# Turning feed-forward activations with 32x32 block transposes and a trip through DRAM

## The chip, the cores and the metric

The kernel runs on one core of a Trainium2 chip. The metric is the device time of one execution in microseconds (us). TensorE (PE) does the matrix products, VectorE (DVE) and ScalarE (ACT) the elementwise work, GpSimd (POOL) a few small operations, and SyncE (SP) issues the DMAs. Sixteen DMA engines move data between DRAM (HBM) and the on-chip memory; all queues share them.

## The reference

Two transformer blocks of two layers each run one after the other on one sequence of 256 positions, width 1024, in fp32. Block 1 has in each layer a SwiGLU feed-forward, a mixer with three attention branches, and a second SwiGLU feed-forward; block 2 has in each layer a mixer with two attention branches and a squared-ReLU feed-forward. What matters here are the feed-forwards:

```
# block 1, four times (width 2816)
g, u = split(h @ w_gu);  x = x + 0.5 * ((silu(g) * u) @ w_down)
# block 2, twice (width 4096)
u = square(relu(h @ w_up));  x = x + gt2 * (u @ w_down)
# once, for block 2: mod = silu(c) @ w_ada + b_ada   (c is one vector)
```

## The kernel before, in words

**Arithmetic.** A product in fp32 is done as three matmuls in a shorter format (fp32r). Each operand is split into a high part (`Copy` on ACT into fp32r) and a low part (original minus high part, on DVE), and PE adds hi x hi, hi x lo and lo x hi (L1238, L1239, L1240).

**Blocks, pieces, units.** Every weight product is a `Block`: 512 output columns (or fewer) and all of K. A block is cut into pieces of two 128-row slices of K; a piece is done for the first half of the tokens (t = 0) and then for the second (t = 1), and each of these is a unit: two slices of three matmuls, six matmuls of 512 columns. Weights arrive in groups of four slices (1 MB) in one of four `raw` buffers (L1132, issued by SP), are split per piece into one of eight `whi` (L1159, ACT) and one of eight `wlo` buffers (L1157, DVE), and the split of a piece is written out six pieces ahead of its use.

**The order of the work** is a stream written out by a generator program. Before each unit, `step()` advances every running chain (a Python generator that writes instructions) by one; `yield n` in a chain means that it goes on n units later. If the activations that a unit needs are not yet written in the program, `step()` is called again until they are (L1224 to L1229). All engines execute in the order of the program, each on its own queue, and wait for each other by semaphores.

**Activations.** The left operand of a product has to have the K dimension on the partitions, so each result of 128 tokens x 512 columns (a strip, for one t) is turned: four 128x128 transposes on PE into one PSUM bank (`transposes`, L206), then `HT.put` writes the high part (ACT, L226) and the low part (DVE, L228). In the SwiGLU a strip j costs two blocks, one for the gate (silu on ACT, L404) and one for the up columns (product on DVE, L409). There are five strips of 512 columns and one of 256, whose gate and up columns share a block. In block 2 the width is done in two parts of 2048 columns; a part has four strips j (relu L1042 and square L1043 on ACT), and then a down product of two blocks over the part's K (added to x at L1024 and L1025). A down block reads strip 0 first, then 1, 2, 3 and so on.

**Chores.** During the feed-forwards of block 1 the program also computes `mod`: 192 loads of 256 KB of `w_ada` on SP's queue (L330), alternately two and three units apart. Each is multiplied into an accumulator on DVE (L345, L347); that instruction is written after the next load's, about five units after its own load.

**Memory.** Temporaries of up to 2 KB per partition come from one pool of 18 slots (`slab2`), taken and given back in the order of the program.

Of the kernel before, what the change touches and what calls it, by code (L numbers as in the profile page):

```python
# [7 lines left out]
F32 = mybir.dt.float32  # L8
F32R = mybir.dt.float32r
BF16 = mybir.dt.bfloat16  # L10
I32 = mybir.dt.int32
AF = mybir.ActivationFunctionType
# [4 lines left out]
D = 1024  # L17
# [7 lines left out]
NBUF = 8  # L25
NRAW = 4
NS4 = 14
NS2 = 18
LEAD = 6
SKEW_2 = 7  # L30
SKEW_1 = 6
# [7 lines left out]
UP_WAIT = 2  # L39
ACT_WAIT = 3  # L40
P_WAIT = 4
MERGE_WAIT = 3
PT_WAIT = 3
ROPE_WAIT = 5
# [20 lines left out]
def tile_kernel(ctx: ExitStack, tc: tile.TileContext, a, out, stages=99):  # L65
    nc = tc.nc
    V, S, T, G = nc.vector, nc.scalar, nc.tensor, nc.gpsimd

    def pool(name, bufs, **kw):
        return ctx.enter_context(tc.tile_pool(name=name, bufs=bufs, **kw))  # L70

    const = pool("const", 1)
# [5 lines left out]
    small = pool("small", 6)  # L78
    mmp = pool("mmp", 3, space=PSUM)
    trp = pool("trp", 5, space=PSUM)  # L80
    dram = pool("dram", 1, space=bass.MemoryType.DRAM)
    ctx.enter_context(tc.manual_schedule())

    def slab4(shape, dt=F32):
# [2 lines left out]
    def slab2(shape, dt=F32):  # L87
        return s2p.tile(shape, dt, name="s2", tag="s2")
# [8 lines left out]
    def bc(ap, shape):  # L97
        return ap.to_broadcast(shape)

    def tk(t):  # L100
        return slice(t * 128, (t + 1) * 128)
# [2 lines left out]
    x = [const.tile([128, D], F32, name=f"x{t}") for t in range(2)]  # L104
    ident = const.tile([128, 128], F32, name="ident")
    cols = const.tile([128, NCOLS], F32, name="cols")
    tri = const.tile([128, 512], F32, name="tri")
    nhalf = const.tile([128, 32], F32, name="nhalf")
    identb = const.tile([128, 128], BF16, name="identb")
    masks = const.tile([128, 5, 128], BF16, name="masks")  # L110
    trir = const.tile([128, 2, 128], F32R, name="trir")
    rope1 = const.tile([128, 2, 2, 16], F32, name="rope1")
# [12 lines left out]
    def setup_late():  # L125
        yield 10
        S.activation(csil, cols[:, COLS["c_2"]:COLS["c_2"] + 8], AF.Silu)
        spawn(chores())
        mk = slab2([128, 3, 128])
        pi = small.tile([128, 2], I32, name="pi")  # L130
        pf = small.tile([128, 2], F32, name="pf")
        inv = small.tile([128, 32], F32, name="inv")
        for dst, src in ((tri, a["tri"]), (mk, a["masks"]), (rope1, a["rope1"]), (pi, a["pos"]), (inv, bc(a["inv"][None, :], [128, 32]))):
            nc.sync.dma_start(out=dst, in_=src)
            yield 2
        for l in range(2):
            for c, n, nm in ((0, 6, "b_forget"), (8, 8, "swa_sinks_2"), (32, 64, "g_idx_k")):
                nc.sync.dma_start(out=rowb[:, l, c:c + n], in_=row(nm, l, n))
                yield 2
        yield 8  # L140
        V.memset(masks[:, 0], 0.0)
        V.tensor_copy(masks[:, 1:3], mk[:, 0:2])
        V.tensor_copy(masks[:, 3], mk[:, 0])
        V.tensor_copy(masks[:, 4], mk[:, 2])
        V.tensor_copy(trir, tri[:, 256:512].rearrange("p (a b) -> p a b", a=2))
        V.tensor_copy(identb, ident)
        for l in range(2):
            V.tensor_scalar(rowb[:, l, 16:24], rowb[:, l, 8:16], -1.0, None, op0=ALU.mult)
        V.tensor_copy(pf, pi)
        w = slab2([128, 3, 2, 32])  # L150
        ang, n, nh = w[:, 0], w[:, 1], w[:, 2]
        for t in range(2):
            V.tensor_scalar(ang[:, t], inv, pf[:, t:t + 1], None, op0=ALU.mult)
        for first in (True, False):
            V.tensor_scalar(n, ang, 0.15915494309189535, MAGIC, op0=ALU.mult, op1=ALU.add)
            V.tensor_scalar(n, n, -MAGIC, None, op0=ALU.add)
            if first:
                V.tensor_scalar(nh, n, 1.0 / 4096, MAGIC, op0=ALU.mult, op1=ALU.add)
                V.tensor_scalar(nh, nh, -MAGIC, 4096.0, op0=ALU.add, op1=ALU.mult)
                V.tensor_sub(n, n, nh)  # L160
            for c in TWO_PI:
                if first:
                    V.scalar_tensor_tensor(ang, nh, -c, ang, op0=ALU.mult, op1=ALU.add)
                V.scalar_tensor_tensor(ang, n, -c, ang, op0=ALU.mult, op1=ALU.add)
            yield 2
        V.tensor_scalar(nh, ang, 1.5707963267948966, None, op0=ALU.add)
        V.tensor_scalar(n, nh, PI, -6.283185307179586, op0=ALU.is_gt, op1=ALU.mult)
        V.tensor_add(nh, nh, n)
        V.tensor_scalar(nh, nh, PI, -PI, op0=ALU.min, op1=ALU.max)
        V.tensor_scalar(ang, ang, PI, -PI, op0=ALU.min, op1=ALU.max)  # L170
        S.activation(sin2[:, :, 0], nh, AF.Sin)
        S.activation(sin2[:, :, 1], ang, AF.Sin)
        spawn(launcher())
# [29 lines left out]
    def transposes(src, n=128):  # L203
        pt = trp.tile([128, 4, 128], F32, name="tr")
        for i, s in enumerate(src):
            T.transpose(pt[:n, i, :], s, ident)  # L206
        return pt

    def chunks(src, k):
        return [src[:, i * 128:(i + 1) * 128] for i in range(k)]  # L210

    class HT:


        def __init__(self, sizes=None):
            self.q, self.done = {}, set()
            self.at = [(i, j) for i, n in enumerate(sizes or [4] * 8) for j in range(n)]

        def tile(self, i):
# [4 lines left out]
        def put(self, i, t, src, n=4):  # L224
            h, l = self.tile(i)
            S.activation(h[:, :n, tk(t)], src, AF.Copy)  # L226
            yield 1
            V.tensor_sub(l[:, :n, tk(t)], src, h[:, :n, tk(t)].bitcast(F32))  # L228
            self.done.add((i, t))

        def ready(self, kc, t):
            return (self.at[kc][0], t) in self.done
# [15 lines left out]
    plan = []  # L248
# [146 lines left out]
    def plan_ffn(l, prep, w_gu, w_down, nxt, before_down=None):  # L395
        sizes = [4, 4, 4, 4, 4, 2]
        aT = HT(sizes)
        for j in range(6):
            n, c0 = sizes[j] * 128, sum(sizes[:j]) * 128
            sg = {}  # L400

            def silu(t, ps, n=n, sg=sg):
                sg[t] = slab2([128, 512])
                S.activation(sg[t][:, :n], ps[:, :n], AF.Silu, scale=prep.r[t])  # L404
                yield

            def mul(t, ps, n=n, sg=sg, j=j):
                act = slab2([128, 512])
                V.scalar_tensor_tensor(act[:, :n], ps[:, :n], prep.r[t], sg.pop(t)[:, :n], op0=ALU.mult, op1=ALU.mult)  # L409
                yield ACT_WAIT  # L410
                pt = transposes(chunks(act, n // 128))
                yield 1
                yield from aT.put(j, t, pt[:, :n // 128], n // 128)

            def both(t, ps, silu=silu, mul=mul):
                yield from silu(t, ps[:, 0:256])
                yield from mul(t, ps[:, 256:512])

            if n == 256:
                plan.append(Block(w_gu[l], D, c0, 512, prep.hT, both, second=DFF + c0))  # L420
            else:
                plan.append(Block(w_gu[l], D, c0, n, prep.hT, silu, skew=SKEW_1 * (j == 0)))
                plan.append(Block(w_gu[l], D, DFF + c0, n, prep.hT, mul))
        if before_down:
            before_down()
        for nh in range(2):
            def add(t, ps, nh=nh):
                xs = x[t][:, nh * 512:(nh + 1) * 512]
                V.scalar_tensor_tensor(xs, ps, 0.5, xs, op0=ALU.mult, op1=ALU.add)  # L429
                yield from nxt.half(t, nh)  # L430

            if nh and nxt.kind == "final":
                plan.append(lambda: busy.append(1))
            plan.append(Block(w_down[l], DFF, nh * 512, 512, aT, add))
# [601 lines left out]
    def plan_mlp2(l, prep, gt, nxt, before_down=None, cuts=(0, 512, 1024)):  # L1036
        for part in range(2):
            uT = HT()
            for j in range(4):
                def up(t, ps, j=j, uT=uT):  # L1040
                    u = slab2([128, 512])
                    S.activation(u, ps, AF.Relu)  # L1042
                    S.activation(u, u, AF.Square)  # L1043
                    yield UP_WAIT
                    pt = transposes(chunks(u, 4))
                    yield 1
                    yield from uT.put(j, t, pt)

                plan.append(Block(a["w_up_2"][l], D, part * 2048 + j * 512, 512, prep.hT, up, skew=SKEW_2 * (part == 0 and j == 0)))
            if part and before_down:  # L1050
                before_down()
            plan_res(a["w_down_2"][l][part * 2048:(part + 1) * 2048], 2048, uT, gt, nxt if part else None, cuts if part else (0, 512, 1024))
# [4 lines left out]
    p = p_ffn[0]  # L1057
    for l in range(2):
# [3 lines left out]
        p = Prep(1, gcol("g_ffn2", l))  # L1062
# [14 lines left out]
        p = q  # L1077
# [38 lines left out]
    i = 0  # L1116
# [190 lines left out]
```

## Time and profile before

| | us |
|---|---|
| median of 3 runs | 1912.08 (1912.01 to 1912.32) |
| the profiled execution, its own time | 1911.74 |
| its span, first to last instruction | 1910.0 |
| PE busy | 1888.1 (99%) |
| DVE busy | 1305.8 (68%) |
| ACT busy | 1040.4 (54%) |
| granted TensorE clock | 1.00 throughout |

Busy time is the time in which an instruction of the engine ran; the issuing of DMAs isn't counted in it. Matmuls overlap each other, so PE's pace is better read from the distances between the starts of its instructions than from their durations. SPq marks the queue of SP, on which a DMA issue has a start and a duration of its own, apart from the time that the transfer takes.

### The profile page before, as it was taken

What the parts mean: (1) busy time and instruction counts of PE and PEld (TensorE: products, weight loads), DVE (VectorE), ACT (ScalarE), POOL (GpSimd) and SP (SyncE); (2) the same over time, 40 slices, a digit from 0 to 9 for tenths busy, and PEclk for the clock granted to TensorE, in tenths of its full rate; (3) what the DMA queues carried; (4) which work ended last, traced back from release to release, by engine and by line L of the source; (5) the groups of instructions that cost most, each with busy time, mean ns of one, the idle gap of its engine ahead of it and who ended that gap; (6) DMA issues with size and microseconds to landing.
All of it is one profiled execution on the core that took longest, in us unless ns stands there. A gap on an engine that the chain in (4) does not pass through costs nothing.

```text
span 1910.0 us, 24975 instructions
## 1 busy us (share of the span) xinstructions
PE 1888.1 (99%) x9300; PEld 1557.6 (82%) x9300; DVE 1305.8 (68%) x2231; ACT 1040.4 (54%) x1622; POOL 68.4 (4%) x84
## 2 busy tenths in 40 slices
PE   8999999999999999999999999999999999999999
PEld 6888987888888888897888888877888887788888
DVE  6876775577677776684757775886855479767454
ACT  5444576555444544466655443677464547656452
POOL 0000100000000000000000000110000012000000
PEclk9999999999999999999999999999999999999999
DMA  9777553558776877563456775644665645456552
GB/s 316 264 266 244 158 170 118 177 184 278 259 262 232 286 250 253 192 186 116 143 193 242 265 264 175 200 154 133 205 214 177 218 138 177 154 177 210 187 165 78
DMA packets 212041, 385.73 MB, mean 202 GB/s; under 512 B 12008, under 2 KB 43752, under 8 KB 211920
## 3 DMA queue, kind: packets, MB, share of 16 engines
q1 hardware_dynamic: 211920, 384.14, 60.3%
q8 instruction: 73, 1.20, 0.3%
q14 instruction: 48, 0.39, 0.1%
HBM read 382.96 MB, written 1.15 MB: 201 GB/s over the span
## 4 chain that ended last, share of the span: by engine, by line
PE 92%; DVE 4%; ACT 3%; issue 1%; DMA 0%; SPq 0%; POOL 0%; ACTq 0%
PE mm L1238 28%; PE mm L1240 28%; PE mm L1239 28%; PE tr L206 4%; PE tr L448 1%; DVE wlo L1157 1%; ACT whi L1159 1%; PE tr L517 1%; PE tr L519 0%; DVE s L903 0%; PE tr L361 0%; DMA x<-in_x_dram 0%; DVE s L852 0%; ACT s L470 0%; ACT s L696 0%
## 5 line engine op out<-in xcount | busy, mean ns | idle before, releaser
L1238 PE MATMUL mm<-whi,s 128*128 128x512 f32 (+3 forms) x2600 | 1011.0, 389 | 1.3 <-ACT s L404 1.2
L1240 PE MATMUL mm<-whi,s 128*128 128x512 f32 (+3 forms) x2600 | 989.2, 380 | 0.4 <-DVE s L228 0.3
L1239 PE MATMUL mm<-wlo,s 128*128 128x512 f32 (+3 forms) x2600 | 987.7, 380 | 1.0 <-DVE wlo L1157 1.0
L1157 DVE TENSOR_TENSOR wlo<-raw,whi 128x1024 fp32r<-128x1024 f32 (+4 forms) x657 | 751.3, 1159 | 281.7 <-ACT whi L1159 279.8
L1159 ACT ACTIVATE whi<-raw 128x1024 fp32r<-128x1024 f32 (+4 forms) x657 | 644.9, 1004 | 267.8 <-PE mm L1240 252.9
L1238 PEld LDWEIGHTS mm<-whi,s 128*128 128x128 f32 x2600 | 489.4, 188 | 98.5 <-issue 13.4
L1240 PEld LDWEIGHTS mm<-whi,s 128*128 128x128 f32 x2600 | 488.8, 188 | 93.0 <-DVE s L228 1.4
L1239 PEld LDWEIGHTS mm<-wlo,s 128*128 128x128 f32 x2600 | 489.7, 188 | 84.2 <-DVE wlo L1157 1.9
L347 DVE SCALAR_TENSOR_TENSOR s<-s,csil,s 128x512 f32<-128x512 f32 x168 | 125.6, 747 | 56.6 <-DMA s<-in_w_ada_dram 56.6
L226 ACT ACTIVATE s<-tr 128x512 fp32r<-128x512 f32 (+1 forms) x112 | 64.3, 580 | 106.0 <-PE tr L206 106.0
L206 PE MATMUL tr<-ident,s 128*128 128x128 f32 x734 | 110.1, 274 | 5.8 <-ACT s L786 2.6
L206 PEld LDWEIGHTS tr<-ident,s 128*128 128x128 f32 x734 | 88.5, 141 | 28.9 <-issue 7.3
L262 ACT ACTIVATE s<-x 128x512 bf16<-128x512 f32 x44 | 27.7, 630 | 124.8 <-DVE x L429 56.4
L228 DVE TENSOR_TENSOR s<-tr,s 128x512 fp32r<-128x512 f32 (+1 forms) x112 | 73.2, 666 | 4.3 <-ACT s L226 3.9
L404 ACT ACTIVATE s<-mm,prep 128x512 f32<-128x512 f32 (+1 forms) x48 | 31.3, 653 | 79.0 <-PE mm L1240 78.0
L409 DVE SCALAR_TENSOR_TENSOR s<-mm,prep,s 128x512 f32<-128x512 f32 (+1 forms) x48 | 33.8, 704 | 43.6 <-PE mm L1240 38.2
L268 POOL TENSOR_TENSOR prep<-prep,nhalf 128x1 f32<-128x1 f32 x18 | 16.9, 937 | 1059.6 <-DVE prep L267 1059.6
L456 DVE CUSTOM_DVE_ANT_0 s<-tr,masks 128x128 f32<-128x128 f32 x88 | 27.7, 353 | 30.4 <-PE tr L448 30.4
L1024 DVE TENSOR_TENSOR s<-mm,s 128x512 f32<-128x512 f32 (+1 forms) x26 | 16.8, 647 | 46.1 <-PE mm L1240 46.1
L1042 ACT ACTIVATE s<-mm 128x512 f32<-128x512 f32 x32 | 19.1, 597 | 41.7 <-PE mm L1240 40.3
L226 ACT ACTIVATE s<-s 128x512 fp32r<-128x512 f32 x24 | 14.9, 630 | 40.9 <-DVE s L317 40.9
L820 ACT ACTIVATE s<-mm,prep 128x512 f32<-128x512 f32 x24 | 16.5, 688 | 34.7 <-PE mm L1240 32.4
(206 smaller groups left out, 900.1 us busy)
## 6 DMA issues: line engine op xcount, KB each, us to landing
raw<-in_w_ffn_gu_dram SPq DMA_DIRECT2D x79, 1024.0 KB, 5.9
raw<-in_w_in_dram SPq DMA_DIRECT2D x56, 1024.0 KB, 5.2
s<-in_w_ada_dram SPq DMA_DIRECT2D x192, 256.0 KB, 5.9
raw<-in_w_ffn_down_dram SPq DMA_DIRECT2D x40, 1024.0 KB, 5.3
raw<-in_w_up_dram SPq DMA_DIRECT2D x32, 1024.0 KB, 5.4
raw<-in_w_down_dram SPq DMA_DIRECT2D x28, 1024.0 KB, 5.2
raw<-in_w_out_dram SPq DMA_DIRECT2D x16, 1024.0 KB, 5.1
raw<-in_w_in_dram SPq DMA_DIRECT2D x16, 640.0 KB, 4.0
```

The costliest lines, as they stand in the source:

```text
L206: T.transpose(pt[:n, i, :], s, ident)
L226: S.activation(h[:, :n, tk(t)], src, AF.Copy)
L228: V.tensor_sub(l[:, :n, tk(t)], src, h[:, :n, tk(t)].bitcast(F32))
L262: S.activation(slab2([128, 512], BF16), x[t][:, nh * 512:(nh + 1) * 512], AF.Square, scale=1.0 / 32, accum_out=self.ms[:, t, o + nh:o + nh ...
L347: V.scalar_tensor_tensor(accs[0], raw, c, accs[0], op0=ALU.mult, op1=ALU.add)
L404: S.activation(sg[t][:, :n], ps[:, :n], AF.Silu, scale=prep.r[t])
L409: V.scalar_tensor_tensor(act[:, :n], ps[:, :n], prep.r[t], sg.pop(t)[:, :n], op0=ALU.mult, op1=ALU.mult)
L1157: V.tensor_sub(lo[:pr, d, :b.n], src, h.bitcast(F32))
L1159: S.activation(h, src, AF.Copy)
L1238: T.matmul(ps, xh, hi[:, i, :b.n], start=(k == 0), stop=False)
L1239: T.matmul(ps, xh, lo[:, i, :b.n], start=False, stop=False)
L1240: T.matmul(ps, xl, hi[:, i, :b.n], start=False, stop=(k == len(b.rows) - 1))
```

## The change

For the strips of 512 columns of the SwiGLU (five of six, four times) and for two of the four strips in each part of block 2's feed-forward, the transposes on PE go. DVE transposes the strip in 32x32 blocks inside the on-chip memory, one instruction for each t; ACT's queue issues a DMA that writes the 256 KB to DRAM. When both t are written, ACT's queue issues four DMAs that read the strip back in the turned order (128 KB each, one for each quarter of the partitions) into one buffer `back`. Then ACT makes the high part and DVE the low part from `back`. `BLOCK_WAITS` holds the distances in units: 2 from the transpose to the write, 9 from the write of t = 1 to the reads, 9 from the reads to the high part. A list `landing` lets one strip at a time be between its reads and its low parts. In block 2 the strips are computed in the order 2, 3, 0, 1, and strips 2 and 3, which the down block reads last, take the new way. To make room, some constants move to the pool, which has 17 slots instead of 18.

```diff
-NS2 = 18
+NS2 = 17
...
+BLOCK_WAITS = (2, 9, 9)
...
+    blocksp = pool("blocksp", 4, space=bass.MemoryType.DRAM)
+    backp = pool("backp", 1)
...
-    tri = const.tile([128, 512], F32, name="tri")
+    tri = const.tile([128, 256], F32, name="tri")
...
+        def put_blocks(self, i, t, src):
+            turned = slab2([128, 512])
+            V.transpose(turned, src.rearrange("p (c j a) -> p j c a", j=4, a=32))
+            if t == 0:
+                self.blocks[i] = blocksp.tile([128, 4, 2, 128], F32, name="d")
+            d = self.blocks[i]
+            yield BLOCK_WAITS[0]
+            nc.scalar.dma_start(out=d[:, :, t], in_=turned.rearrange("p (j e) -> p j e", j=4))
+            if t == 0:
+                return
+            yield BLOCK_WAITS[1]
+            while landing:
+                yield 1
+            landing.append(1)
+            back = backp.tile([128, 4, 2, 128], F32, name="back")
+            for j in range(4):
+                nc.scalar.dma_start(out=back[32 * j:32 * j + 32], in_=self.blocks[i].rearrange("(i a) j t e -> j a i (t e)", a=32)[j])
+            yield BLOCK_WAITS[2]
+            h, l = self.tile(i)
+            for u in range(2):
+                x_, hu, lu = back[:, :, u].rearrange("p i (c s) -> p c i s", s=32), *(z[:, :, tk(u)].rearrange("p c (i s) -> p c i s", s=32) for z in (h, l))
+                S.activation(hu, x_, AF.Copy)
+                yield 1
+                V.tensor_sub(lu, x_, hu.bitcast(F32))
+                self.done.add((i, u))
+            landing.clear()
...
             def mul(t, ps, n=n, sg=sg, j=j):
                 act = slab2([128, 512])
                 V.scalar_tensor_tensor(act[:, :n], ...)
+                if n == 512:
+                    yield 1
+                    yield from aT.put_blocks(j, t, act)
+                    return
                 yield ACT_WAIT
...
-            for j in range(4):
+            for j in (2, 3, 0, 1):
                 def up(t, ps, j=j, uT=uT):
                     u = slab2([128, 512])
                     S.activation(u, ps, AF.Relu)
                     S.activation(u, u, AF.Square)
                     yield UP_WAIT
+                    if j > 1:
+                        yield from uT.put_blocks(j, t, u)
+                        return
                     pt = transposes(chunks(u, 4))
```

## Rows read from the trace of the kernel before

**Rows 1.** Head of the page: span; busy time, share of the span, instructions.

```profile
span 1910.0 us, 24975 instructions
PE 1888.1 (99%) x9300; PEld 1557.6 (82%) x9300; DVE 1305.8 (68%) x2231; ACT 1040.4 (54%) x1622; POOL 68.4 (4%) x84
```

**Rows 2.** Chain that ended last, share of the span by engine.

```profile
PE 92%; DVE 4%; ACT 3%; issue 1%; DMA 0%; SPq 0%; POOL 0%; ACTq 0%
```

**Rows 3.** What PE waited for, whole span: total us, times, longest.

```profile
PE mm L1239 <- DVE wlo L1157: 1.0, 1, 1.0
```

**Rows 4.** Timeline of ACT, second feed-forward: start, duration, instruction, idle before and releaser.

```profile
531.55 1.06 ACT L1159 ACTIVATE whi<-raw 128x1024 fp32r<-128x1024 f32 x1 [1.66 <-PE mm L1240]
```

**Rows 5.** Timeline of PE around one group of four transposes, first feed-forward.

```profile
61.62 0.40 PE L1240 MATMUL mm<-whi,s 128*128 128x512 f32 x1
61.86 0.60 PE L206 MATMUL tr<-ident,s 128*128 128x128 f32 x4
62.21 0.48 PE L1238 MATMUL mm<-whi,s 128*128 128x512 f32 x1
62.53 0.40 PE L1239 MATMUL mm<-wlo,s 128*128 128x512 f32 x1
```

**Rows 6.** Timeline of DVE, feed-forward of block 2, layer 0.

```profile
1410.66 0.68 DVE L228 TENSOR_TENSOR s<-tr,s 128x512 fp32r<-128x512 f32 x1
...
1422.48 0.68 DVE L228 TENSOR_TENSOR s<-tr,s 128x512 fp32r<-128x512 f32 x1
...
1440.44 0.69 DVE L1024 TENSOR_TENSOR s<-mm,s 128x512 f32<-128x512 f32 x1 [4.48 <-PE mm L1240]
...
1462.20 0.69 DVE L1024 TENSOR_TENSOR s<-mm,s 128x512 f32<-128x512 f32 x1 [4.48 <-PE mm L1240]
```

**Rows 7.** Groups by shape: count, total busy us, mean ns, idle before.

```profile
L228 DVE TENSOR_TENSOR s<-tr,s 128x512 fp32r<-128x512 f32 x104 | 69.8, 685 | 4.3 <-ACT s L226 3.9
L226 ACT ACTIVATE s<-tr 128x512 fp32r<-128x512 f32 x104 | 61.2, 595 | 97.2 <-PE tr L206 97.1
L228 DVE TENSOR_TENSOR s<-s,s 128x512 fp32r<-128x512 f32 x24 | 16.2, 688 | 5.1 <-ACT s L226 4.9
L226 ACT ACTIVATE s<-s 128x512 fp32r<-128x512 f32 x24 | 14.9, 630 | 40.9 <-DVE s L317 40.9
L345 DVE TENSOR_SCALAR s<-s,csil 128x512 f32<-128x512 f32 x24 | 11.6, 483 | 6.0 <-DMA s<-in_w_ada_dram 6.0
```

**Rows 8.** Stretches: busy us by engine, clock, DMA share, GB/s (strips 1 to 5; start).

```profile
410.00:530.00 120.00, 120.00 (x558) 98.60 (x557) 87.94 (x104) 61.55 (x74) 2.04 (x2) 1.00 0.73 249
15.00:17.50 2.50, 2.50 (x14) 2.09 (x13) 2.50 (x4) 1.75 (x4) 0.00 (x0) 1.00 1.06 387
```

**Rows 9.** Timeline of SP's queue, second feed-forward: issues.

```profile
544.34 0.38 SPq L1132 DMA_DIRECT2D raw<-in_w_ffn_down_dram  x1
544.83 0.92 SPq L330 DMA_DIRECT2D s<-in_w_ada_dram  x2
```

**Rows 10.** The same at the start of the kernel.

```profile
15.70 11.19 SPq L1132 DMA_DIRECT2D raw<-in_w_ffn_gu_dram  x4
```

**Rows 11.** DMA issues: count, KB each, median us from issue to landing.

```profile
s<-in_w_ada_dram SPq DMA_DIRECT2D x192, 256.0 KB, 5.9
...
out_dram<-x SPq DMA_DIRECT2D x4, 128.0 KB, 1.7
```

**Rows 12.** Timeline of ACT, feed-forward of block 2: relu and square of a strip.

```profile
1417.74 0.60 ACT L1042 ACTIVATE s<-mm 128x512 f32<-128x512 f32 x1 [3.02 <-PE mm L1240]
1418.37 0.63 ACT L1043 ACTIVATE s<-s 128x512 f32<-128x512 f32 x1
```

**Rows 13.** What DVE waited for between 410 and 530 us.

```profile
DVE wlo L1157 <- ACT whi L1159: 10.2, 7, 3.2
DVE s L409 <- PE mm L1240: 9.7, 3, 4.5
DVE s L347 <- DMA s<-in_w_ada_dram: 7.9, 5, 3.5
```

More of the change, by code (lines that the diff above doesn't have):

```diff
@@ L129, in setup_late @@
         mk = slab2([128, 3, 128])
[L130 to L133, printed above, removed]
+        pi = slab2([128, 2], I32)
+        late = slab2([128, 2, 128])
+        pfi = slab2([128, 34])
+        pf, inv = pfi[:, 0:2], pfi[:, 2:34]
+        for dst, src in ((tri, a["tri"][:, 0:256]), (late, a["tri"][:, 256:512].rearrange("p (a b) -> p a b", a=2)), (mk, a["masks"]), (rope1, a["rope1"]), (pi, a["pos"]), (inv, bc(a["inv"][None, :], [128, 32]))):
             nc.sync.dma_start(out=dst, in_=src)
@@ L144, in setup_late @@
         V.tensor_copy(masks[:, 4], mk[:, 2])
-        V.tensor_copy(trir, tri[:, 256:512].rearrange("p (a b) -> p a b", a=2))
+        V.tensor_copy(trir, late)
         V.tensor_copy(identb, ident)
@@ L210, in chunks @@
         return [src[:, i * 128:(i + 1) * 128] for i in range(k)]
+    landing = []
     class HT:
         def __init__(self, sizes=None):
-            self.q, self.done = {}, set()
+            self.q, self.done, self.blocks = {}, set(), {}
             self.at = [(i, j) for i, n in enumerate(sizes or [4] * 8) for j in range(n)]
@@ L1047, in up @@
                     yield from uT.put(j, t, pt)
-                plan.append(Block(a["w_up_2"][l], D, part * 2048 + j * 512, 512, prep.hT, up, skew=SKEW_2 * (part == 0 and j == 0)))
+                plan.append(Block(a["w_up_2"][l], D, part * 2048 + j * 512, 512, prep.hT, up, skew=SKEW_2 * (part == 0 and j == 2)))
             if part and before_down:
```

## The prediction

> **What bounds the kernel now.** I read the head of the page first: PE is busy for 1888.1 of 1910.0 us, DVE for 68% and ACT for 54% [rows 1]. Busy matmuls can hide waiting, so I looked next at the chain that ended last: 92% of it is PE [rows 2]. Then at what PE waits for: a low weight part was late once in the whole span, by 1.0 us [rows 3]. And then at ACT, which feeds DVE: in the steady stream it finishes a `whi` and stands 1.66 us until PE gives a buffer back [rows 4]. So the splits run as far ahead as the buffers let them, and the time is the sum of what PE executes. What takes instructions off PE is worth its full length, as long as the others still keep ahead.
>
> **Part 1: the transposes that go.** Between the starts of the last matmul before a group of four and the second one after it lie 0.91 us [rows 5]; without the group it would be two steps. A step I take from a down block without transposes: the two halves of x, one block of 16 units apart, lie at 1440.44 and 1462.20, so 21.76 us for 16 units or 1.36 for a unit of six matmuls, 0.227 each [rows 6]. The group costs 0.91 - 0.45 = 0.46. The other way: two strips of block 2 in succession are 11.82 us apart (1410.66 to 1422.48) and hold 8 units and two groups [rows 6]: (11.82 - 10.88) / 2 = 0.47. I take 0.47.
> Groups that go: 5 strips x 2 t x 4 SwiGLUs = 40, and 2 strips x 2 t x 2 parts x 2 layers = 16; together 56, so PE loses 56 x 0.47 = 26.3 us.
> The Trainium skill speaks against it: "VectorE: DVE Perf Modes", Rules for kernel authors, sends a 128x128 transpose to TensorE and keeps DVE's for 32x32 blocks, and its section on the three transpose paths gives 390 ns for one on TensorE (bf16). Here four take 0.47 us in fp32, so the row is cheaper than the page; by its figure 56 x 4 x 0.39 = 87 us would go. The rule leaves out that PE is the only full engine here, and the row decides.
>
> **Part 2: DVE.** It gains 56 block transposes; the two low parts of a strip stay, from memory instead of PSUM (688 against 685 ns) [rows 7]. No row shows a block transpose. The nearest from below is a one-source operation of the same shape, 483 ns; from above two passes of a two-stream one, 2 x 688 = 1.38 us [rows 7]. I take 0.69, one element a step as in the two-stream rows. In the strips of a SwiGLU DVE is busy for 87.94 of 120 us [rows 8]. A strip takes 16 x 1.36 + 2 x 0.47 = 22.70 us now, 16.6 of them busy; afterwards 16.6 + 2 x 0.69 = 18.0 of 21.76 (83%), or 19.4 (89%) at the upper bound. It is off the path either way, at 0 us.
>
> **Part 3: ACT.** The high parts cost 630 instead of 595 ns [rows 7], 2 us in all, hidden. New are the issues on its queue: 2 writes and 4 reads for each of 28 strips, 168. No row shows an issue on ACT. SP's take 0.38 us for 1 MB and 0.46 for 256 KB [rows 9]; with 4 MB queued at the start they took 11.19 / 4 = 2.8 [rows 10]. I take 0.46, since the stream in between is the first kind, and keep 2.8 as the far end; the lower end is 0. ACT in a strip: 61.55 / 120 x 22.70 = 11.6 us, then 11.6 + 6 x 0.46 = 14.4 of 21.76; it keeps its lead. At 2.8 it would be 28.4 and ACT the bound (below).
>
> **Part 4: are the activations in time?** In units after the end of a strip's t = 1 (U) the program of the SwiGLU writes: product at 1, block transpose at 2, DMA write at 4, reads at 13, high part at 22, low parts at 23 and 24. The last strip of this kind has 8 units of strip 5 and 16 units of the down block in front of it and is needed from U + 25: two units to spare at t = 0 and at t = 1. The write waits on ACT for DVE's transpose only, and the reads wait for the write. A store of 128 KB landed after 1.7 us [rows 11]; nine units are 12.2 us, so neither wait holds up the `whi` queued behind it. The next strip's reads come at 29, when `landing` is empty since 24. Cost 0.
> The Trainium skill, "DMA: Bandwidth & Descriptors", section on two DMAs through the same engine, says that only the first one's completion makes it safe to read what it wrote; the 1.7 us row is that completion for half the bytes, and no run here shows the read behind it.
> In block 2 it is tighter. Relu and square at 1, transpose 3, write 5, reads 14, low parts 24 and 25; strip 3 finds `landing` taken until U + 25 of strip 2, so its reads are written in the very unit in which strip 1's t = 1 is evicted, and in front of it on ACT. They also wait for DVE's last low part of strip 2, because there is one `back`. Relu and square start up to 1.8 us (four issues) and about 1 us for that low part late, and PE's transposes of strip 1 are written only two units (2.72 us) behind, of which relu and square need 1.23 [rows 12]. So 2.8 + 1.23 - 2.72 = 1.3 us of PE wait, once in the second part of each layer: 2 x 1.3 = 2.6. In the first part seven pieces are skewed, the collision falls on the high part of strip 1, which has four units until it is read, and strip 3's low part is written one `step()` late, both behind data already landed: 0. Without the new order strips 2 and 3 would be the ones next to the down block; with it strip 1 keeps PE's transposes and is ready one unit ahead.
>
> **Part 5: the small edits.** The constants move at the start, on SP, where PE waits for x and weights; the pool with 17 slots, now with `turned` held until its write has landed, can make a later user wait. No row prices that: between -1 and +2 us, since the one wait of PE above is of that size [rows 3]; I take 0.
>
> **Sum.** 1911.74 (the profiled execution) - 26.3 + 2.6 = 1888.0; the median of the runs shown lies 0.34 above that execution, so 1888.4 in the terms of the median. Forecast 1888.5, with a range of its own from 1885 to 1893.
>
> **Rivals.**
> A. *ACT's issues cost more than SP's, or the read data come late.* For it: ACT would execute them between splits, which SP doesn't do, and no row shows it. At 1.2 us each a burst of four is 4.8 instead of 1.8, so each of the four parts of block 2 loses about 3 us more, 12 in all: 1888.5 + 12 = 1900.5. Against it: the strips of block 1 have two units to spare and ACT 7 us of each strip.
> B. *Slower: the chores' loop in the SwiGLUs becomes the bound.* SP takes its next load when DVE has finished a `wlo`; the `w_ada` load behind it lands, and DVE stands at the accumulation, written about five units after the load. DVE waits there now: 7.9 us of the 120, while the waits that show it ahead (for `whi` and for PE's results) are 19.9 [rows 13]. A leg is 0.38 + 0.92 + 5.9 = 7.2 us [rows 9, 11], and after it one to three units of DVE's work until the next load of a group of weights. With loads of weights every 4 and chores every 2 and 3 units the tightest round of 40 units has five legs and 11 units of work between them: 5 x 7.2 + 11 x 18.0 / 16 = 48.4 us against PE's 54.4. So a landing later by 1.2 us makes the loop PE's equal. The new traffic, 1 MB for each strip, lifts 249 GB/s [rows 8] to 249 x 22.70 / 21.76 + 48 = 308; 387 were reached when the queue was full [rows 8], so it fits, but bursts meet. The lead of the splits, six pieces or 16.3 us, is spent first in each SwiGLU. To eat the gain of 26.3 the loop must lose 16.3 + 6.6 in each of four stretches of 120 us, which is 5 x (later - 1.2) = 10.4 us a round: landing 3.3 us later, at 9.2. At 9.7 it is 5 x 2.6 / 54.4 x 120 - 16.3 = 12.4 us in each of four: 1888.5 + 49.6 = 1938. The same side is reached if an issue on ACT costs 2.8 us [rows 10]: (28.4 - 21.76) x 20 strips = 133 us.
> C. *No change.* The same loop with a landing at 9.2, or strips late by 0.94 us each: 28 x 0.94 = 26, the whole gain, 1912. Against it: the spare units of part 4.
>
> **How the numbers follow.** Forecast 0.62. A, gain cut to between 5 and 20 us: 0.23. C 0.06, B 0.09. Faster by more than 0.2% (3.8 us, about what a measurement of this kernel can tell from no change): 0.62 + 0.23 = 0.85; same 0.06; slower 0.09. The range for 8 in 10 goes from 1885 (all of part 1, nothing lost) to 1900, which takes most of A; the rest of A, and C and B, are left out above.
>
> **What would show it.** Right: no L206 groups on the strips, two strips of a SwiGLU 21.76 us apart; ACT still standing before `whi` for PE; DVE's transposes near 0.69 us; in block 2 a wait of PE of about a us before strip 1's transposes in each second part. Wrong: PE waiting for low parts (of weights: B; of activations, in strip 4 of a SwiGLU or 2 and 3 of block 2: A), landings of `w_ada` above 7 us, ACT issues far above 0.46.

## The result, and the profile after

The kernel after the change takes 1925.82 us (median of four runs, 1922.14 to 1929.62) against 1912.05 (four runs of the kernel before, 1911.82 to 1912.32): a ratio of 1.0069, 95% interval 1.0058 to 1.0081. It is slower by 13.8 us where 23.6 less were forecast. The head of its page and its chain, beside [rows 1, 2]:

```profile
span 1924.9 us, 24852 instructions
PE 1874.8 (97%) x9076; PEld 1540.0 (80%) x9076; DVE 1337.3 (69%) x2287; ACT 1036.2 (54%) x1622; POOL 67.9 (4%) x84
...
PE 74%; DMA 10%; DVE 9%; ACT 3%; issue 2%; SPq 1%; POOL 0%; DVEq 0%; ACTq 0%
PE mm L1280 23%; PE mm L1282 22%; PE mm L1281 22%; DMA s<-in_w_ada_dram 8%; DVE wlo L1199 4%; PE tr L210 3%; DMA d<-s 1%; PE tr L487 1%; DVE s L382 1%; ACT whi L1201 1%; PE tr L556 1%; DVE s L262 1%; DVE s L444 1%; DMA raw<-in_w_ffn_gu_dram
```

PE does execute 224 instructions less (56 groups of four), yet its share of the chain fell from 92% to 74%, and loads of `w_ada`, which PE never reads, hold 8% of it. The line numbers have moved: L1280 to L1282 are the three matmuls (before L1238 to L1240), L444 is the product (before L409), L382 and L380 the accumulation of `w_ada` (L347, L345), L1199 and L1201 the low and high parts of the weights, L891 an eviction in block 1's mixer (L852). What PE waited for, and then DVE (total us, times, longest), beside [rows 3, 13], and last the two rows of DVE's in the kernel before, for the whole span:

```profile
PE mm L1280 <- DVE s L444: 25.7, 14, 3.5
...
PE mm L1280 <- DVE s L891: 2.7, 1, 2.7
...
PE mm L1281 <- DVE wlo L1199: 1.0, 1, 1.0
```

```profile
DVE wlo L1199 <- ACT whi L1201: 219.0, 131, 6.3
DVE s L382 <- DMA s<-in_w_ada_dram: 114.9, 58, 4.5
...
DVE s L380 <- DMA s<-in_w_ada_dram: 18.5, 8, 6.3
```

```profile
DVE s L347 <- DMA s<-in_w_ada_dram: 56.6, 38, 4.3
...
DVE s L345 <- DMA s<-in_w_ada_dram: 6.0, 6, 2.4
```

PE's wait for a low part is the same single 1.0 us as before: the weights never became late. What is new is that PE waits for DVE's product, which reads a finished PSUM bank and so frees it. DVE stands 133.4 us at the accumulation (114.9 and 18.5), where it stood 62.6 before. One of the 14 stops, first DVE's timeline, then PE's (start, duration, instruction, idle before and releaser):

```profile
127.64 0.75 DVE L382 SCALAR_TENSOR_TENSOR s<-s,csil,s 128x512 f32<-128x512 f32 x1 [4.54 <-DMA s<-in_w_ada_dram]
128.31 2.35 DVE L1199 TENSOR_TENSOR wlo<-raw,whi 128x1024 fp32r<-128x1024 f32 x2
...
135.53 0.75 DVE L382 SCALAR_TENSOR_TENSOR s<-s,csil,s 128x512 f32<-128x512 f32 x1 [3.33 <-DMA s<-in_w_ada_dram]
136.20 0.74 DVE L444 SCALAR_TENSOR_TENSOR s<-mm,prep,s 128x512 f32<-128x512 f32 x1
```

```profile
133.99 0.39 PE L1282 MATMUL mm<-whi,s 128*128 128x512 f32 x1
137.00 0.50 PE L1280 MATMUL mm<-whi,s 128*128 128x512 f32 x1 [2.62 <-DVE s L444]
...
139.27 0.63 PE L1281 MATMUL mm<-wlo,s 128*128 128x512 f32 x1
139.70 0.63 PE L1282 MATMUL mm<-whi,s 128*128 128x512 f32 x1
140.12 0.63 PE L1280 MATMUL mm<-whi,s 128*128 128x512 f32 x1
```

Two waits for a load within 8 us; the product stands behind the second one in DVE's queue, though its input had been there since about 131.7 (it carries no wait of its own); PE stops 2.62 us. From 138.4 to 141.4 its matmuls then start every 0.43 us instead of 0.227. The stretches around it show why (busy us by engine, granted clock, DMA share, GB/s):

```profile
130.00:135.00 5.00, 4.38 (x20) 3.29 (x18) 2.20 (x3) 2.10 (x3) 0.00 (x0) 1.00 1.03 263
135.00:140.00 5.00, 3.00 (x9) 2.44 (x10) 4.47 (x7) 0.70 (x1) 0.00 (x0) 0.81 0.58 201
140.00:145.00 5.00, 5.00 (x20) 4.00 (x20) 4.87 (x6) 3.42 (x5) 0.00 (x0) 0.85 0.99 349
145.00:150.00 5.00, 5.00 (x24) 4.14 (x23) 4.49 (x8) 2.00 (x4) 0.00 (x0) 1.00 0.75 240
```

The granted clock is 0.81 and 0.85 after the stop: for part of these 10 us PE ran at 1.2 instead of 2.4 GHz, which cost 0.19 and 0.15 of 5 us, 1.7 us. The same 1.7 us (a clock of 0.83 over 10 us) follows the stops for the product at 61.6, 557.1 and 1127.5 and the one for the mixer's eviction at 952.9, together 8.5 us. After the other ten stops for the product the clock stayed at 1.00, after one of 2.95 us at 112.3 too; the kernel before had 1.00 throughout. The Trainium skill, "TensorE: Matmul & The Clock Gate", Part 1, says that a clock gate follows how busy PE was; these rows agree with it.

Where each stage stands, from the starts of DVE's first update of x after each (169.6 in the kernel before and 178.8 after for the first feed-forward, and so on): the four SwiGLUs of block 1 took +9.2, +2.3, +2.7 and +3.5 us, though ten groups of 0.47 had gone from each; the first mixer 0.0, the second +4.3; the four parts of block 2's feed-forwards -1.8, -1.9, -1.8 and -1.9; nothing else moved. Together +14.6 of the span's 14.9.

Three theories stood against each other. T (traffic): the new traffic makes `w_ada` land later, DVE stands at the accumulation, PSUM comes free late. Q: the cause is ACT, which stands behind its own DMA issues. V: DVE is simply too full.

### The profile page after: what moved, and what is told of

Same layout as the page of the kernel before. It is cut to its first block, busy times and chain, and to the rows that moved or that the text cites. A ratio compares the mean times of both kernels' runs of the same rounds, so it can differ in the third digit from the quotient of the medians.

```text
span 1924.9 us, 24852 instructions
## 1 busy us (share of the span) xinstructions
PE 1874.8 (97%) x9076; PEld 1540.0 (80%) x9076; DVE 1337.3 (69%) x2287; ACT 1036.2 (54%) x1622; POOL 67.9 (4%) x84
## 4 chain that ended last, share of the span: by engine, by line
PE 74%; DMA 10%; DVE 9%; ACT 3%; issue 2%; SPq 1%; POOL 0%; DVEq 0%; ACTq 0%
PE mm L1280 23%; PE mm L1282 22%; PE mm L1281 22%; DMA s<-in_w_ada_dram 8%; DVE wlo L1199 4%; PE tr L210 3%; DMA d<-s 1%; PE tr L487 1%; DVE s L382 1%; ACT whi L1201 1%; PE tr L556 1%; DVE s L262 1%; DVE s L444 1%; DMA raw<-in_w_ffn_gu_dram 0%; SPq L1174 0%
## 5 line engine op out<-in xcount | busy, mean ns | idle before, releaser
L1280 PE MATMUL mm<-whi,s 128*128 128x512 f32 (+3 forms) x2600 | 1010.8, 389 | 29.6 <-DVE s L444 25.7
L1282 PE MATMUL mm<-whi,s 128*128 128x512 f32 (+3 forms) x2600 | 991.5, 381 | 0.3 <-DVE s L234 0.3
L1199 DVE TENSOR_TENSOR wlo<-raw,whi 128x1024 fp32r<-128x1024 f32 (+4 forms) x657 | 748.4, 1157 | 220.0 <-ACT whi L1201 219.0
L1201 ACT ACTIVATE whi<-raw 128x1024 fp32r<-128x1024 f32 (+4 forms) x657 | 642.9, 1004 | 360.7 <-PE mm L1282 194.4
L1280 PEld LDWEIGHTS mm<-whi,s 128*128 128x128 f32 x2600 | 490.9, 189 | 136.0 <-DVE s L444 31.6
L1282 PEld LDWEIGHTS mm<-whi,s 128*128 128x128 f32 x2600 | 490.8, 189 | 93.3 <-DVE s L234 1.7
L382 DVE SCALAR_TENSOR_TENSOR s<-s,csil,s 128x512 f32<-128x512 f32 x168 | 125.6, 747 | 115.3 <-DMA s<-in_w_ada_dram 114.9
L210 PE MATMUL tr<-ident,s 128*128 128x128 f32 x510 | 76.4, 275 | 5.8 <-ACT s L825 2.7
L210 PEld LDWEIGHTS tr<-ident,s 128*128 128x128 f32 x510 | 60.7, 141 | 21.1 <-issue 6.5
L232 ACT ACTIVATE s<-tr 128x512 fp32r<-128x512 f32 (+1 forms) x56 | 30.7, 562 | 54.6 <-PE tr L210 41.4
L303 POOL TENSOR_TENSOR prep<-prep,nhalf 128x1 f32<-128x1 f32 x18 | 16.4, 912 | 1070.6 <-DVE prep L302 1070.6
L241 DVE STREAM_TRANSPOSE s<-s 128x512 f32<-128x512 f32 x56 | 39.6, 707 | 11.7 <-ACT s L1082 11.3
L234 DVE TENSOR_TENSOR s<-tr,s 128x512 fp32r<-128x512 f32 (+1 forms) x56 | 35.2, 647 | 5.4 <-ACT s L232 5.1
L262 DVE TENSOR_TENSOR s<-back,s 128x512 fp32r<-128x512 f32 x56 | 36.8, 684 | 0.0
```

Of the source, the lines that this page charges most:

```text
L241: V.transpose(turned, src.rearrange("p (c j a) -> p j c a", j=4, a=32))
L262: V.tensor_sub(lu, x_, hu.bitcast(F32))
L382: V.scalar_tensor_tensor(accs[0], raw, c, accs[0], op0=ALU.mult, op1=ALU.add)
L1199: V.tensor_sub(lo[:pr, d, :b.n], src, h.bitcast(F32))
L1201: S.activation(h, src, AF.Copy)
L1280: T.matmul(ps, xh, hi[:, i, :b.n], start=(k == 0), stop=False)
```

## The experiments

Each time is a median, and every ratio is against runs of the kernel before on the same chip.

**e1: the six block DMAs issued by GpSimd** (Q).

```diff
-            nc.scalar.dma_start(out=d[:, :, t], ...)
+            nc.gpsimd.dma_start(out=d[:, :, t], ...)
```

The four reads likewise.

> The changed kernel with its 168 block DMAs issued by GpSimd instead of ACT; nothing else. Theory Q (queues): ACT's read issues wait for loads that SP has only just issued (the eight completion semaphores go round over both queues), ACT's splits stop behind them, and everything after follows; with GpSimd issuing, ACT no longer stands, and the time is 1886 to 1895. Theory T (traffic): the added 29 MB in small packets fill the DMA engines, w_ada lands late and DVE stands; the traffic is the same, so 1915 to 1930. Theory V (DVE's own queue): DVE with the block transposes and with the waits for w_ada is too late for PE's products even without any of that; 1915 to 1930.

1930.67 us, ratio 1.0090 (1.0069 to 1.0110), 0.7 above the range of T and V. DVE's wait for `w_ada` grew to 139.3 + 23.2 us, PE's for the product was 23.0 after 25.7. With ACT's queue clear of DMAs the loss is still there: Q falls as the cause of this loss.

**e2: no trip.** Block transposes on DVE stay, no write and no read; high and low parts are made from the strip as DVE left it.

```diff
-            nc.scalar.dma_start(out=d[:, :, t], ...)
...
+            x_ = turned.rearrange("p (a b) -> p a b", a=4)
+            S.activation(h[:, :, tk(t)], x_, AF.Copy)
```

> The changed kernel without the trip: high and low parts are made straight from the block-transposed strip, 2 units after the transpose; no write, no reads, so the blocks aren't put in place and the product is another one. ACT and DVE execute as many operations as in the changed kernel. Theories Q and T: PE loses its 26.3 us and nothing stands, 1884 to 1889, with DVE's waits for w_ada near the 63 us of before. Theory V: the FFNs of block 1 stay slow, 1905 to 1925.

1896.15 us, ratio 0.9914 (0.9899 to 0.9929), between the range of Q and T and that of V. DVE has the same transposes, and waits 63.8 + 5.3 us for `w_ada`; three of the four SwiGLUs are 4.7, 4.7 and 4.3 us shorter than before, the first is 0.9 longer, with one stop of 4.2 us for the product. That 0.9 in place of a gain of 4.7, and 4.3 us in the second mixer, of which e5 tells, are what Q and T had not counted. V falls: without traffic DVE's load takes back nothing in three of four, and the whole is 16 us faster.

**e3: the accumulation two loads behind its issue** instead of one, all else as in the change.

```diff
+ACC_LAG = 2
...
-                    if raw is not None:
-                        accumulate(*raw)
+                    if len(queue) > ACC_LAG:
+                        accumulate(*queue.pop(0))
```

> The changed kernel with one edit: a chore's accumulation is written one more load later (two loads behind instead of one), so DVE asks for w_ada some 2.5 units (3.4 us) later. All theories say that DVE stands less at w_ada than the 133 us of the changed kernel. Theory T: landings of 6.6 us are then covered, 1888 to 1898. Theory Q: ACT still stands behind the reads (55 us in the changed kernel), but with DVE's loop loose SP is earlier too; 1895 to 1912. Theory V: 1888 to 1898.

1895.24 us, ratio 0.9911 (0.9896 to 0.9925), granted clock 1.0, faster than both kernels. The number lies in the range of all three theories (Q's begins at 1895), so the waits have to tell. The traffic is all there, ACT's issues too; DVE waits 10.2 + 1.8 us for `w_ada` instead of 133.4, and PE's waits for evictions are

```profile
PE mm L1282 <- DVE s L446: 2.9, 3, 1.6
PE mm L1282 <- DVE s L893: 2.7, 1, 2.7
```

L446 is the product: 2.9 us in place of 25.7. The wait in DVE's queue carries the loss. (L893 is the mixer's eviction, of which e5 tells.)

**e4: block 2 only.** The SwiGLUs keep PE's transposes; all small edits stay.

```diff
-                if n == 512:
+                if n == 0:
```

> Only block 2's strips 2 and 3 take the new way; the SwiGLUs keep PE's transposes. There are no chores in block 2. All theories: the 16 groups go at 0.47 us each, 7.5 us less than before: 1904 to 1906. If the edits around it (17 slots, constants in the pool) cost something in block 1 it is 1906 to 1912.

1910.98 us, ratio 0.9991 (0.9982 to 1.0001). Block 2's parts gain 1.7, 1.9, 1.7 and 1.9 us as in the change, but 6.3 us go elsewhere: 1.9 in the first SwiGLU and 4.4 in the second mixer of block 1, where nothing is changed but the slots and the moved constants. That is the second branch of the expectation, 1906 to 1912.

**e5: the kernel before with 17 slots,** one number changed.

```diff
-NS2 = 18
+NS2 = 17
```

> The kernel before with 17 instead of 18 slots of 2 KB and nothing else. Theory S (the one slot taken away is what the block-2-only kernel lost: there the second mixer's softmax waited 4.62 us for a transposed matmul of PE before its next slot was free, DVE and ACT stood behind it, an eviction came late and PE stopped 2.69 us, with a granted clock of 0.66 in the 5 us after): the same PE stop of about 2.7 us in the second mixer, that mixer 4.4 us longer, the first feed-forward 0 to 1.9 us longer: 1916 to 1918.5 us. Rival K (the loss comes from the constants that went into slots at the start, or from block 2's new order): 1911.5 to 1912.8 us and no such stop.

1916.49 us, ratio 1.0024 (1.0015 to 1.0033): S holds, the second mixer is 4.5 us longer. The first SwiGLU isn't (-0.4), so e4's 1.9 us there are not the slot's; of what e4 changes in block 1 only the moved constants are left, which weren't tried alone. The slot's chain can be read in two engines. DVE's timeline in the second mixer (L456 writes the scores of a head into a slot), first of the kernel before, then of e5:

```profile
921.96 0.08 DVE L456 DVE_READ_ACCUMULATOR2_ANT st<- 128x1 f32 x1
...
922.15 0.28 DVE L456 CUSTOM_DVE_ANT_0 s<-tr,masks 128x128 f32<-128x128 f32 x1
```

```profile
926.49 0.29 DVE L456 CUSTOM_DVE_ANT_0 s<-tr,masks 128x128 f32<-128x128 f32 x1 [4.62 <-PE tr L519]
...
937.69 0.68 DVE L852 TENSOR_TENSOR s<-mm,s 128x512 f32<-128x512 f32 x1
```

With 18 slots the second head's scores follow at once; with 17 they wait 4.62 us for the slot that PE's matmul at L519 still reads. The softmax comes late, ACT's and DVE's work behind it too, the eviction L852 last, and PE stops, with a lower granted clock after it:

```profile
938.43 0.50 PE L1238 MATMUL mm<-whi,s 128*128 128x512 f32 x1 [2.69 <-DVE s L852]
```

```profile
935.00:940.00 5.00, 2.31 (x9) 1.54 (x8) 3.30 (x4) 5.00 (x10) 0.00 (x0) 0.93 0.01 5
940.00:945.00 5.00, 5.00 (x21) 3.28 (x20) 4.11 (x6) 4.78 (x8) 0.00 (x0) 0.73 0.64 210
```

2.69 us stopped and 0.07 and 0.27 of 5 us each, 1.7, lost to the clock make 4.4.

**e6: the traffic alone.** PE's transposes stay; the strips are also written and read back as they are, and the result of the reads is not used.

```diff
-            turned = slab2([128, 512])
-            V.transpose(turned, src.rearrange("p (c j a) -> p j c a", j=4, a=32))
+            turned = src
...
-                    yield from aT.put_blocks(j, t, act)
-                    return
+                    spawn(aT.put_blocks(j, t, act))
```

> The kernel after, but with PE's transposes and the direct evictions kept; the writes and reads through DRAM are issued all the same, from the strips as they are, and what they bring back is not used. No 32x32 transposes on DVE. Theory T (the traffic alone makes the loads of w_ada land later, DVE stands at the accumulation, PSUM comes free late, PE stops): PE waits for DVE's product in the SwiGLU parts many times, DVE waits over 90 us for w_ada, time 1925 to 1945 us. Rival J (traffic and the added 0.7 us transposes on DVE are needed together): no more than the small edits' 6 us, 1916 to 1920 us.

1924.82 us, ratio 1.0066 (1.0051 to 1.0082), 0.2 below T's range and above J's. DVE's wait for `w_ada` rose to 103.3 + 16.4 us, as T wants, but PE waited for the product only three times, 4.9 us. With the slot's 4.4 taken off (1916.49), the traffic alone costs 8.3 us, in the first and the last SwiGLU (+6.1, +1.9); the change, counted from the 18.8 us that its four SwiGLUs should have gained, lost 36.5. So T is one part of it: the traffic makes DVE late, and something that e6 leaves out turns that into many more stops. It leaves out two things, PE's faster strips and the added transposes on DVE, and no run separates them.

**e7: the kernel before with the accumulation two loads behind,** the edit of e3.

> The kernel before with the accumulation of w_ada two loads behind its issue instead of one, and nothing else. Theory T: in the kernel before, DVE stood 62.6 us at these accumulations but PE never waited for DVE's product, so nothing is to be had: 1911.5 to 1912.5 us, with DVE's wait for w_ada near 0. Rival (late accumulation is worth something by itself, so that its gain in the changed kernel says nothing of the traffic): below 1908 us.

1911.96 us, ratio 0.9998 (0.9989 to 1.0007). DVE's wait falls from 62.6 to 4.2 us and nothing is gained: in the kernel before the wait was covered, and only the change makes it matter.

**e8: e3 with 18 slots,** for which the landing place is one tile of 2 KB and one slot, read by eight DMAs.

```diff
-            back = backp.tile([128, 4, 2, 128], F32, name="back")
+            back = [backp.tile([128, 4, 128], F32, name="back"), slab2([128, 4, 128])]
```

> The changed kernel with the accumulation two loads behind and with 18 slots again; to fit, the landing place is one tile of 2 KB and one borrowed slot, so eight reads of 512-byte runs take the place of four of 1024-byte runs. Theory S with T: the second mixer's 4.1 us come back and perhaps part of the first feed-forward's 3.2 us: 1888 to 1891.5 us. Rival (twice the reads, 8 x 0.35 us of issue per pair on ACT, or the borrowed slot, bring a stop of their own): 1894 to 1900 us.

1967.58 us, ratio 1.0284 (1.0270 to 1.0298): far outside every expectation. What ACT waited for, and its timeline in the first SwiGLU:

```profile
ACT whi L1204 <- PE mm L1285: 184.4, 121, 8.5
ACT whi L1204 <- DMA s<-d: 71.1, 9, 11.3
```

```profile
49.28 0.36 ACTq L257 DMA_DIRECT2D back<-d  x1
49.40 1.05 ACT L1204 ACTIVATE whi<-raw 128x1024 fp32r<-128x1024 f32 x1
49.68 2.67 ACTq L257 DMA_DIRECT2D back<-d  x3
56.19 5.18 ACTq L257 DMA_DIRECT2D s<-d  x4
61.49 1.06 ACT L1204 ACTIVATE whi<-raw 128x1024 fp32r<-128x1024 f32 x1 [11.04 <-DMA s<-d]
```

The issues need 0.36 us each, but the later ones wait in ACT's queue for the landing of earlier ones: the kernel has eight completion semaphores for the DMAs of SP and ACT together, and each issue first waits for the DMA eight before it. With eight reads on end, reads of the same strip are among these. The splits of the weights stand behind them for 11.04 us. This is Q's mechanism: it is real, four reads (e9) keep it small, eight don't. The borrowed slot, the other thing in which e8 differs from e9, wasn't tried alone. The Trainium skill, "DMA: Bandwidth & Descriptors", Anatomy of one DMA — SWDGE (gpsimd) path, says that a DMA engine doesn't wait for semaphores and the issuing engine does; the 11.04 us agree.

**e9: e3 with 18 slots and four reads,** the landing place in one of the 14 slots of 4 KB.

```diff
-NS2 = 17
+NS2 = 18
...
-            back = backp.tile([128, 4, 2, 128], F32, name="back")
+            back = slab4([128, 4, 2, 128])
```

> The changed kernel with the accumulation two loads behind, 18 slots again, and the four reads as in the change; the landing place is one of the 14 slots of 4 KB. Theory S with the reading of the eight-read kernel (there ACT stood 71 us behind its own reads, up to 11.3 us at once, and the weights' splits with it; the slots had nothing to do with it): the second mixer's 4.1 us come back, 1890 to 1892 us, and DVE's wait for whi as with two loads behind and 17 slots. Rival L (the lent slot of 4 KB or the 18th slot does harm by itself): 1894 to 1950 us, with waits of the strips' writers for their slots.

1889.63 us, ratio 0.9885 (0.9869 to 0.9902), 0.4 below the expected 1890 to 1892 and the fastest kernel here. The second mixer is as before the change (+0.1), the SwiGLUs gain 1.1, 4.7, 4.7 and 4.6 us and block 2's parts 1.9 each. The busy row of strips 1 to 5 in the second SwiGLU, for [rows 8]:

```profile
410.00:530.00 120.00, 120.00 (x541) 98.56 (x540) 92.88 (x112) 61.58 (x73) 2.03 (x2) 1.00 0.91 290
```

DVE at 92.88 of 120, DMA share 0.91 instead of 0.73, and PE is busy for all of it at full clock. Single loads of `w_ada` land as late as 11.0 us after their issue here (9.5 in the change), and PE doesn't feel it.

**e10 and e11: e9 and e3 with the block DMAs on GpSimd** (the edit of e1).

> The same with the six block DMAs issued by GpSimd, so that no read stands ahead of a weight split on ACT. If ACT's standing still costs something once the accumulation is out of the way: the first feed-forward comes 1 to 3 us nearer to the full 4.7 us, 1887.5 to 1890 us. If not: the same as with the issues on ACT within 1 us.

> The changed kernel with the accumulation two loads behind and the six block DMAs issued by GpSimd, 17 slots as in the change. The second mixer keeps its 4.1 us; ACT's standing as in the expectation before it: 1892 to 1894.5 us if it costs something, 1894.5 to 1896 us if it doesn't.

1891.26 us, ratio 0.9889 (0.9874 to 0.9904), and 1894.85, ratio 0.9910 (0.9895 to 0.9925). e10 lies 1.6 us above e9, so past the "within 1 us" by a little and not on the side of a gain; e11 is within 0.4 of e3. With four reads, taking the issues off ACT wins nothing back. That ACT's standing is free isn't shown by it, since DVE's wait for `w_ada` is longer with GpSimd (35.4 us in e10, 10.8 in e9).

**e12: the change with 18 slots,** the accumulation one load behind as it was (e9's edit without e3's).

> The changed kernel with 18 slots again (landing place in one of the slots of 4 KB) and the accumulation one load behind as it was. Additive reading: the slot costs 4.4 us in the second mixer and nothing else, the wait for w_ada the rest: 1919 to 1922.5 us, DVE's wait for w_ada above 100 us and PE's stops for DVE's product as in the changed kernel (over 20 us together). Rival (the 17th slot was also what made the accumulation's wait harmful, since its loads sit in these slots): below 1910 us.

1924.30 us, ratio 1.0063 (1.0047 to 1.0080), above the expected 1919 to 1922.5. In its profiled execution (1920.2) the second mixer is 0.0 and the product's stops are there:

```profile
PE mm L1279 <- DVE s L443: 24.6, 17, 4.2
```

So the slot is not what makes the accumulation harmful. That the two costs add up can't be read from the medians, since the runs of a kernel with these stops scatter more (1920.20 to 1926.93) than the slot is worth.

## Why the prediction was wrong

Two terms that were put at 0 failed. Part 2 took DVE to be "off the path either way, at 0 us": in the four SwiGLUs DVE stood at the accumulation with PE's evictions behind it, and that cost most of a gap of 36.5 us. Part 5 took the small edits at 0: the slot cost 4.4 us.

**What bounds the kernel: right for before, wrongly carried over.** "The splits run as far ahead as the buffers let them" is true and stayed true: the 1.0 us wait for a low part never grew. But the splits are only one thing that PE needs from DVE. The other is the eviction of a PSUM bank, and for that no lead of weights helps. I read DVE's accumulation waits [rows 13] as something that DVE could afford, without asking what else stood behind them in its queue.

**Part 1: right.** The three clean SwiGLUs of e9 gain 4.6 to 4.7 us for ten groups and block 2's parts 1.9 for four: 0.47 each, as taken.

**Part 2: the price right, "off the path at 0" wrong.** The transposes and the low parts, whole span, for [rows 7]:

```profile
L241 DVE STREAM_TRANSPOSE s<-s 128x512 f32<-128x512 f32 x56 | 39.6, 707 | 11.7 <-ACT s L1082 11.3
L262 DVE TENSOR_TENSOR s<-back,s 128x512 fp32r<-128x512 f32 x56 | 36.8, 684 | 0.0
```

707 ns for 690. Their busy time alone does no harm in three of the four SwiGLUs (e2), but a mean share (83% forecast, 77% in e9's row) says nothing of an engine that stands 4.5 us at a time.

**Part 3: right for the issues.** 0.35 us for a read and 0.52 for a write, for 0.46. GpSimd instead wins nothing.

**Part 4: the SwiGLU wrong, block 2 right but for 2.6 us.** In block 2 the collision came as written: four reads in front of strip 1's relu, which starts 1.25 us late (ACT's timeline, second part, layer 0):

```profile
1527.65 1.76 ACTq L255 DMA_DIRECT2D back<-d  x4
1529.46 0.60 ACT L1081 ACTIVATE s<-mm 128x512 f32<-128x512 f32 x1 [1.25 <-issue]
```

DVE's last low part had already been read out of `back`, so the added "about 1 us" was not there. The relu was 1.25 us late instead of 2.8, and 1.25 + 1.23 is less than 2.72, so PE had nothing to wait for; in layer 1, with 1.60, PE shows no wait there either. For the landing of the write I had taken 1.7 us, from the four stores at the end of the kernel; under load writes took 6.8 and reads 6.5 (medians, the store's row being [rows 11]):

```profile
s<-in_w_ada_dram SPq DMA_DIRECT2D x192, 256.0 KB, 6.6
...
d<-s ACTq DMA_DIRECT2D x56, 256.0 KB, 6.8
back<-d ACTq DMA_DIRECT2D x112, 128.0 KB, 6.5
```

Nine units still cover them. "Neither wait holds up the `whi`" did not hold: `whi` stood 63.9 us behind writes that waited for DVE's transpose. DVE's standing at the accumulation is only a part of that, as e3 still has 42.5. PE didn't wait for weights in either.

**Part 5: "I take 0", wrong.** The slot costs 4.4 us (e5), outside the bounds of -1 to +2; those came from a wait in another place. The right question was which instruction takes the 18th slot, and what waits behind it.

**Rival B named the place, with the wrong price.** It had SP's load, the landing and DVE's stand in it, but let the loop hurt only through the weights, so that six pieces or 16.3 us had to be spent first and `w_ada` to land at 9.2. What failed is this step: the loss began at a median landing of 6.6 (before 5.9; the longest that the trace records 9.5, before 8.1), through the evictions. For these there are three PSUM banks, and in the stop shown they gave 2.7 us: the product's input was there at 131.7, and PE stood at 134.4. So none of the signs that the prediction named for being wrong came: PE waited for low parts of weights no longer than before (1.0 us) and for none of the strips', the median landing stayed below 7 us, and ACT's issues took 0.35 and 0.52 us. The bill of the four SwiGLUs: 18.8 us forecast as gain, 17.7 lost, a gap of 36.5; 25.7 of it PE's stops for the product, 6.8 the lower clock after four of them; some 4 us are not placed. The first SwiGLU gives 1.1 instead of 4.7 us in e9 too, with 2.4 us of stops for the product, and loses 0.9 in e2; why it alone keeps some stays open. The moved constants are a candidate: e4, in which the SwiGLUs keep PE's transposes, loses 1.9 us there, with one stop of 1.1 us for the product.

With both causes taken out, e9's 1889.63 lies 1.1 us from the forecast of 1888.5. That it is so near is partly luck: the 3.6 us that the first SwiGLU still misses stand against the 2.6 that part 4 charged and block 2 didn't cost. The price of a group, 0.47 us, was right, for a kernel that the change is not.

## What to carry to other kernels

Before taking work off a full engine, list for each engine that serves it everything that stands in the same in-order queue, and look for waits with spare time now: an instruction that waits for a DMA in front of a PSUM eviction is harmless only as long as the banks cover it. Traffic that fits the bandwidth can still make the landings of other loads later (in the change a median of 6.6 us for 5.9, the longest 9.5 for 8.1); put the users of such loads one more load behind, which cost nothing here and turned +0.7% into -0.9%. One slot less in a shared pool is an edit with a price, to be looked for where the pool runs full.

## What was not expected of the hardware

A stop of PE of 2.6 to 2.7 us cost about 1.7 us more in the two that were followed up, as the granted clock was 0.73 to 0.93 in the 5 us stretches after it. Not every stop had that price: the clock fell after a stop of 1.79 us at 61.6 and not after one of 2.95 us at 112.3. A DMA issue on ACT took 0.35 us to execute, but up to 11.04 us of standing when eight followed each other. Issuing the same 168 DMAs from GpSimd changed the time by no more than the runs scatter once the accumulation was moved (1894.85 for 1895.24).
